# A hybrid residual block on one core: squares and scaling moved from GpSimd to ScalarE and VectorE, the memory heads' steps one chunk later

## The chip, the cores and the metric

The kernel runs on one core of one Trainium2 chip. A core has five engines, each with an instruction queue of its own that runs in order: TensorE (PE, matmuls into PSUM banks), VectorE (DVE, elementwise), ScalarE (ACT, elementwise with a function), GpSimd (POOL) and SyncE (SP, which here only issues DMAs). They wait for one another through semaphores. The metric is the device time of one execution in microseconds (us); lower is better.

## The reference, cut to what matters

One layer of a residual block, sequence 512, width 2048, float32, with 256 memory tokens. Only the parts that the change touches are spelled out.

```python
def rms_norm(x, g):
    return x * rsqrt(mean(x * x, -1) + 1e-6) * g

h = rms_norm(x, norm_g)                      # 512 x 2048
proj = h @ w_in                              # split into conv, latent attention, memory and gate columns
# branch A: short gated convolution; branch B: latent attention, 16 heads
# branch C: cross-attention into the memory tokens, 4 heads of width 256
q = rms_norm(mem_q.reshape(b, s, 4, 256), mem_qn_g)
k, v = split(rms_norm(mem, mem_norm_g) @ w_mem_kv, 2)
k = rms_norm(k.reshape(b, m, 4, 256), mem_kn_g)
p = softmax(einsum("bqhd,bmhd->bhqm", q, k) / 16)
mem_y = einsum("bhqm,bmhd->bqhd", p, v.reshape(b, m, 4, 256))
# every branch times silu(its gate columns), projected, merged by sigmoid gates, projected by w_o, added to x
```

## The kernel before, in words

Every float32 product is made of three matmuls on reduced-precision parts. A tile is split into `hi` (ScalarE, a copy to the reduced type) and `lo` (VectorE, the tile minus `hi`). `split` (L121) does this for activations, with a gain per partition folded in where there is one; `weights` (L137) does it for a weight chunk of 128x1024. `mm3` (L150) issues hi·hi, hi·lo and lo·hi. So PE cannot begin a chunk before ScalarE has made its `whi`, nor get beyond the first matmuls before VectorE has made its `wlo`. There are two `whi` and two `wlo` buffers and four raw weight buffers, so a `whi` also waits for PE to finish the chunk two places earlier.

**The front** is the stage from the start to the first latent projection. It computes the memory keys and values: four groups of eight weight chunks (32 chunks), each chunk 12 matmuls of 128x512. Three side jobs are woven in:

- In the first eight chunks `memory_chunk` (L248) loads two blocks of the memory tokens, splits them (tiles `mh` and `ml`), and calls `add_squares` (L236), which squares them (tile `sq`) and adds them up in `macc`. `memory_scale` (L261) turns `macc` into the tokens' scale.
- In chunks 6 to 13 `load_x` (L280) loads two blocks of x and adds their squares up in `xacc`.
- From chunk 17 on each step runs one step of `make_hT` (L287): a block of x times the row scale (tile `xs`, L304), then a `split` with the norm gain into the tile `hT`.

Before the change GpSimd squares the memory blocks (L242), adds both kinds of squares (L246) and makes `xs` (L304); ScalarE squares x (L244). GpSimd also takes every reciprocal root as a power of minus a half (L197, L269), on a few columns; these stay. In the front the order on SyncE is the program's; on the other engines the framework orders the instructions itself by a timeline model of its own. The same holds for the latent attention after it.

**The planned part**, from the second memory query group on, is ordered by hand. `drive` (L804) goes through a list of chunks. For each chunk number c it runs, in this order: the hooks set for c (`at`), the splits of the next chunks (`prep`, here for chunk c+1), the steps set for c (`phases`), the postponed pieces whose turn it is (`later`), and then chunk c's own matmuls. The emission order is the order on every engine.

Chunks 0 to 7 are the second memory query group, chunks 8 to 15 the first group of the memory gate, chunks 16 to 23 the second. `query_parts` (L1212) splits the four banks of a finished query group, squares them on ScalarE (`sq`, L1222) and adds the squares of a head on GpSimd (L1224). It is set for chunk 0 (heads 0 and 1) and chunk 8 (heads 2 and 3). `attention` (L1305) sets the steps of a pair of heads: `query_scales` (L1229, sums of `sq` by narrow matmuls at L1234, then the power on GpSimd) and `head_scores` (L1242) of the first head, its softmax as a postponed piece, `head_turn` (L1274, transposes of the softmax), `head_values` (L1287) together with the scores of the second head, and so on. With the pair set at chunk c, these run at c+1 to c+5. Results are copied (`my`) and stored to DRAM from ScalarE's queue one chunk later (L1301). At chunk 15 (`CLOSE`, `switch`, L1344) the memory heads' buffers are given up, and new tiles are laid over them, among them the `y` tiles that are loaded at chunk 15 (L1203 by way of L1326).

Of the kernel before, what the change touches and what calls it, by code (L numbers as in the profile page):

```python
# [20 lines left out]
AF = mybir.ActivationFunctionType  # L21
ALU = mybir.AluOpType
# [16 lines left out]
KC = 2  # L39
# [55 lines left out]
def body(ctx, tc, a, out):  # L95
    nc = tc.nc
    act, vec, pool = nc.scalar, nc.vector, nc.gpsimd
# [23 lines left out]
    def split(src, hi, lo, g=None):  # L121
        act.activation(hi, src, AF.Copy, scale=1.0 if g is None else g)  # L122
        if g is None:
            vec.tensor_tensor(out=lo, in0=src, in1=r32(hi), op=ALU.subtract)  # L124
        else:
            vec.scalar_tensor_tensor(out=lo, in0=src, scalar=g, in1=r32(hi),  # L126
                                     op0=ALU.mult, op1=ALU.subtract)
# [104 lines left out]
    macc = pst.tile([P, KC, M], F32, name="macc")  # L232
    xacc = pst.tile([P, KC, S], F32, name="xacc")
    mT = []

    def add_squares(c, t, acc, eng):  # L236

        sq = acc
        if c:
            sq = pst.tile(list(t.shape), F32, tag="sq", name="sq", bufs=2)  # L240
        if eng is pool:
            pool.tensor_tensor(out=sq, in0=t, in1=t, op=ALU.mult)  # L242
        else:
            act.activation(sq, t, AF.Square)  # L244
        if c:
            pool.tensor_tensor(out=acc, in0=acc, in1=sq, op=ALU.add)  # L246

    def memory_chunk(c):  # L248


        t = pst.tile([P, KC, M], F32, tag="mraw", name="mraw", bufs=4)
        nc.sync.dma_start(t, a["memT"][:, c * KC:(c + 1) * KC])
        for kk in range(KC):
            k = c * KC + kk
            hi = pmt.tile([P, M], F32R, name=f"mh{k}")
            lo = pmt.tile([P, M], F32R, name=f"ml{k}")
            split(t[:, kk], hi, lo, g(G_MEM + k))
            mT.append((hi, lo))
        add_squares(c, t, macc, pool)

    def memory_scale():  # L261
        b = bank("aux")
# [15 lines left out]
    xraws = []  # L278

    def load_x():  # L280
        c = len(xraws)
        t = pht.tile([P, KC, S], F32, tag="hT", name="xraw", bufs=KB + 1)
        nc.sync.dma_start(t, a["xT"][:, c * KC:(c + 1) * KC])
        xraws.append(t)
        add_squares(c, t, xacc, act)

    def make_hT():  # L287


        b = bank("aux")  # L290
        for i in range(NTB):
            for kk in range(KC):
                nc.tensor.matmul(b[:, i:i + 1], lhsT=xacc[:, kk, i * P:(i + 1) * P], rhs=one,
                                 start=kk == 0, stop=kk == KC - 1)
        r = rstd_of(b[:, :NTB], NTB, 1.0 / D, pst)
        rows = pst.tile([P, NTB, P], F32, name="xrows")
        vec.tensor_copy(rows, r.unsqueeze(2).to_broadcast([P, NTB, P]))
        b = transpose4([rows[:, i] for i in range(NTB)])
        scale = pst.tile([P, S], F32, name="xscale")
        act.activation(scale, b, AF.Copy)  # L300
        for k in range(KB):
            t = pht.tile([P, 2, S], F32R, tag="hT", name="hT", bufs=KB + 1)
            xs = pst.tile([P, S], F32, tag="xs", name="xs", bufs=2)
            pool.tensor_tensor(out=xs, in0=xraws[k // KC][:, k % KC], in1=scale, op=ALU.mult)  # L304
            split(xs, t[:, 0], t[:, 1], g(G_NORM + k))
            htiles.append(t)
            hT.append((t[:, 0], t[:, 1]))
            yield
# [5 lines left out]
    for grp in range(4):  # L314
# [12 lines left out]
        if grp < 2:  # L327
            krow = []
            for i, b in enumerate(banks):
                sq = pmt.tile([P, M], F32, tag="ksq", name="ksq")  # L330
# [9 lines left out]
            for f2 in range(2):  # L340
                b = bank("aux")
                for ff in range(2):
                    for i in range(2):
                        f = 2 * f2 + ff
                        nc.tensor.transpose(out=b[:, ff * M + i * P:ff * M + (i + 1) * P],
                                            in_=krow[i][:, f * P:(f + 1) * P], identity=ident)
                for ff in range(2):
                    f = 2 * f2 + ff
# [117 lines left out]
    for i, b in enumerate(banks):  # L466
        sq = pcr.tile([P, 512], F32, tag="csq", name="csq")
        ss = pcr.tile([P, 2], F32, tag="css2", name="css2", bufs=4)
        act.activation(sq[:, :288], b[:, :288], AF.Square, accum_out=ss[:, 0:1])
        t = pcr.tile([P, 512], F32, tag="crow", name="crow", bufs=4)  # L470
# [10 lines left out]
    for i, b in enumerate(banks):  # L481
        sq = pcr.tile([P, 512], F32, tag="csq", name="csq")
# [265 lines left out]
    plan, at, phases = [], defaultdict(list), defaultdict(list)  # L748
# [3 lines left out]
    def later(delay, us, fn):  # L752
        seq[0] += 1
        todo.append((now[0] + delay, seq[0], us, fn))
# [444 lines left out]
    mydram = dram.tile([8, P, S], F32, name="mydram")  # L1199
# [29 lines left out]
    def query_scales(grp):  # L1229

        b = bank(HEADS_IN[grp])
        for h in range(2):
            for i in range(NTB):
                nc.tensor.matmul(b[:, 4 * h + i:4 * h + i + 1], lhsT=heads[2 * grp + h]["sq"][:, i * P:(i + 1) * P],  # L1234
                                 rhs=one, start=True, stop=True)
        r = rstd_of(b[:, :8], 8, 1.0 / M, ppq)
        rs = ppq.tile([P, 8], F32, tag="rs", name="rs", bufs=2)
        vec.tensor_scalar(out=rs, in0=r, scalar1=MEM_SCALE, scalar2=None, op0=ALU.mult)
        for h in range(2):
            heads[2 * grp + h]["rs"] = rs[:, 4 * h:4 * h + 4]  # L1240

    def head_scores(head):  # L1242
        hd = heads[head]
        hd["p"] = []
        sbs = []
        for i2 in range(2):
            sb = bank(HEADS_IN[head // 2])
            for ii in range(2):
                cols = slice((2 * i2 + ii) * P, (2 * i2 + ii + 1) * P)
                for f in range(2):  # L1250
                    mm3(sb[:, ii * M:(ii + 1) * M], (hd["q"][f][0][:, cols], hd["q"][f][1][:, cols]),
                        mkT[2 * head + f], f == 0, f == 1)
            sbs.append(sb)

        def softmax(i2):
            sb, rs = sbs[i2], hd["rs"][:, 2 * i2:2 * i2 + 2]
            mx = ppq.tile([P, 2], F32, tag="mx", name="mx", bufs=2)
            vec.tensor_reduce(out=mx, in_=sb.rearrange("p (a b) -> p a b", a=2), op=ALU.max, axis=AX.X)
            nm = ppq.tile([P, 2], F32, tag="nm", name="nm", bufs=2)
            vec.scalar_tensor_tensor(out=nm, in0=mx, scalar=-1.0, in1=rs, op0=ALU.mult, op1=ALU.mult)  # L1260
            sm = ppq.tile([P, 2], F32, tag="sm", name="sm", bufs=2)
            p = ppq.tile([P, 2, M], F32, tag="p", name="p", bufs=2)
            for ii in range(2):
                act.activation(p[:, ii], sb[:, ii * M:(ii + 1) * M], AF.Exp, scale=rs[:, ii:ii + 1],
                               bias=nm[:, ii:ii + 1], accum_out=sm[:, ii:ii + 1])
            ri = ppq.tile([P, 2], F32, tag="ri", name="ri", bufs=2)
            vec.reciprocal(ri, sm)
            for ii in range(2):
                vec.tensor_scalar(out=p[:, ii], in0=p[:, ii], scalar1=ri[:, ii:ii + 1], scalar2=None, op0=ALU.mult)
                hd["p"].append(p[:, ii])  # L1270
        for i2 in range(2):
            later(0, 1.8, lambda i2=i2: softmax(i2))

    def head_turn(head):  # L1274
        hd = heads[head]
        bs = [transpose4([t[:, j * P:(j + 1) * P] for t in hd["p"]], HEADS_IN[head // 2]) for j in range(2)]
        hd["pt"] = []

        def parts_(j):
            hi = ppq.tile([P, S], F32R, tag=f"ph{j}", name=f"ph{j}")  # L1280
            lo = ppq.tile([P, S], F32R, tag=f"pl{j}", name=f"pl{j}")
            split(bs[j], hi, lo)
            hd["pt"].append((hi, lo))
        for j in range(2):
            later(0, 0.69, lambda j=j: parts_(j))

    def head_values(head):  # L1287
        hd, (grp, h) = heads[head], divmod(head, 2)
        bs = []
        for f in range(2):  # L1290
            yb = bank(HEADS_IN[grp])
            c0 = h * M + f * P
            for j in range(2):
                v = mv[j][grp]
                mm3(yb, (v[0][:, c0:c0 + P], v[1][:, c0:c0 + P]), hd["pt"][j], j == 0, j == 1)
            bs.append(yb)

        def put(f):
            y = ppq.tile([P, S], F32, tag="my", name="my", bufs=2)
            act.activation(y, bs[f], AF.Copy)  # L1300
            later(1, 0, lambda: nc.scalar.dma_start(mydram[2 * head + f], y))  # L1301
        for f in range(2):
            later(0, 0, lambda f=f: put(f))

    def attention(grp, c):  # L1305

        phases[c + 1] += [lambda: query_scales(grp), lambda: head_scores(2 * grp)]
        phases[c + 2] += [lambda: head_turn(2 * grp)]
        phases[c + 3] += [lambda: head_values(2 * grp), lambda: head_scores(2 * grp + 1)]
        phases[c + 4] += [lambda: head_turn(2 * grp + 1)]  # L1310
        phases[c + 5] += [lambda: head_values(2 * grp + 1)]

# [576 lines left out]
```

## Time and profile before

| | |
|---|---|
| median of 3 runs | 2176.95 us (2176.28 to 2177.11) |
| the profiled execution | 2177.01 us |
| its span, first to last instruction | 2175.2 us |
| TensorE clock granted, mean | 0.995 |
| HBM read and written | 269.41 MB and 48.23 MB |

So 1.8 us of the profiled execution lie outside the span. In the page, "busy" is time in which an engine executed something; in the list of groups, the time after the bar is idle time of that engine just before these instructions, and what ended it. A matmul's row shows a duration that includes its drain, so that neighbours overlap: the distance from start to start is what one costs when they follow one another.

### The profile page before, as it was taken

Reading aid. Unit: us, or ns where it says so; the run is one execution under the profiler, and the core shown is the slowest. Engines: PE = TensorE matmul, PEld = TensorE weight load, DVE = VectorE, ACT = ScalarE, POOL = GpSimd, SP = SyncE. Lnnn points to the kernel's source line nnn. Section 1 sums busy time; section 2 is a strip of 40 time slices with the busy share of each in tenths; the row PEclk is TensorE's granted clock in tenths of the full one; section 3 lists DMA queues with packets and bytes.
Section 4 is the critical chain, followed back from the end, with each engine's and each line's share of the span. In section 5 each row is a group of like instructions: output and inputs, shape, how many; then the busy total and the mean of one; then the engine's idle time right before and its main releaser. Section 6 shows DMA issues by size and latency. Waiting matters only on the chain.

```text
span 2175.2 us, 31867 instructions
## 1 busy us (share of the span) xinstructions
PE 2128.4 (98%) x12504; PEld 1893.9 (87%) x12504; DVE 1579.5 (73%) x2200; ACT 1028.1 (47%) x1551; POOL 216.2 (10%) x231
## 2 busy tenths in 40 slices
PE   7999999999999999999999999999999999999999
PEld 5788888888778999999999999888888888888887
DVE  7863777774335878788787776777777778867987
ACT  5533667675333444444444454444445434434433
POOL 7410311210001000000000000000000100111000
PEclk9999999999999999999999999999999999999999
DMA  7473212234227633333434433354344865487462
GB/s 263 159 257 108 88 49 74 68 135 166 70 78 225 205 116 106 120 105 107 141 126 175 164 121 113 117 174 145 98 154 144 282 213 186 147 276 214 152 190 94
DMA packets 110119, 322.35 MB, mean 148 GB/s; under 512 B 13200, under 2 KB 13456, under 8 KB 109968
## 3 DMA queue, kind: packets, MB, share of 16 engines
q1 hardware_dynamic: 78480, 253.89, 34.5%
q0 software_dynamic: 9888, 27.79, 4.7%
q10 hardware_dynamic: 21600, 38.63, 4.7%
q8 instruction: 98, 1.61, 0.3%
q14 instruction: 53, 0.43, 0.1%
HBM read 269.41 MB, written 48.23 MB: 146 GB/s over the span
## 4 chain that ended last, share of the span: by engine, by line
PE 88%; DVE 4%; ACT 3%; issue 2%; DMA 2%; POOL 1%; ACTq 0%; DVEq 0%; POOLq 0%
PE acc L154 15%; PE acc L153 15%; PE acc L155 15%; PE aux L154 13%; PE aux L153 13%; PE aux L155 13%; DVE wlo L147 1%; DVE wlo L124 1%; PE aux L660 1%; PE aux L204 1%; POOL xs L304 1%; ACT whi L122 0%; DVE hT L126 0%; ACT whi L146 0%; PE aux L640 0%
## 5 line engine op out<-in xcount | busy, mean ns | idle before, releaser
L124 DVE TENSOR_TENSOR wlo<-raw,whi 128x1024 fp32r<-128x1024 f32 x440 | 538.8, 1225 | 345.0 <-ACT whi L122 330.1
L122 ACT ACTIVATE whi<-raw 128x1024 fp32r<-128x1024 f32 x440 | 466.1, 1060 | 670.1 <-PE acc L154 159.9
L147 DVE TENSOR_TENSOR wlo<-raw,whi 128x1024 fp32r<-128x1024 f32 (+3 forms) x97 | 119.1, 1229 | 93.6 <-ACT whi L146 92.3
L146 ACT ACTIVATE whi<-raw 128x1024 fp32r<-128x1024 f32 (+3 forms) x97 | 92.7, 956 | 122.6 <-PE acc L155 43.4
L1203 POOL DMA_DIRECT2D y<-gdram x48 | 26.4, 550 | 1197.8 <-DMA gdram<-gy 954.9
L153 PE MATMUL acc<-whi,blk 128*128 128x512 f32 (+1 forms) x352 | 132.5, 380 | 2.0 <-DVE qt L585 1.4
L155 PE MATMUL acc<-whi,blk 128*128 128x512 f32 (+1 forms) x352 | 131.4, 374 | 0.0
L154 PE MATMUL acc<-wlo,blk 128*128 128x512 f32 (+1 forms) x352 | 131.1, 373 | 0.1
L1108 DVE TENSOR_TENSOR raw<-raw 128x1024 f32<-128x1024 f32 x96 | 116.9, 1218 | 0.0
L1018 DVE TENSOR_TENSOR raw<-raw 128x1024 f32<-128x1024 f32 x96 | 116.9, 1218 | 0.0
L122 ACT ACTIVATE whi<-s 128x1024 fp32r<-128x1024 f32 x64 | 67.9, 1062 | 93.9 <-PE acc L155 21.5
L153 PE MATMUL acc<-f,whi 128*128 128x256 f32 x384 | 108.7, 283 | 0.0
L154 PE MATMUL acc<-f,whi 128*128 128x256 f32 x384 | 108.7, 283 | 0.0
L155 PE MATMUL acc<-f,wlo 128*128 128x256 f32 x384 | 108.7, 283 | 0.0
L153 PE MATMUL aux<-f,whi 128*128 128x256 f32 x384 | 108.7, 283 | 0.0
L154 PE MATMUL aux<-f,whi 128*128 128x256 f32 x384 | 108.7, 283 | 0.0
L155 PE MATMUL aux<-f,wlo 128*128 128x256 f32 x384 | 108.7, 283 | 0.0
L154 PE MATMUL acc<-blk,whi 128*128 128x256 f32 (+1 forms) x320 | 97.6, 305 | 0.6 <-DVE blk L124 0.6
L153 PE MATMUL acc<-blk,whi 128*128 128x256 f32 (+1 forms) x320 | 97.8, 306 | 0.0
L153 PE MATMUL acc<-hU,whi 128*128 128x256 f32 (+1 forms) x320 | 97.5, 305 | 0.0
L153 PE MATMUL aux<-blk,whi 128*128 128x256 f32 (+1 forms) x320 | 97.5, 305 | 0.0
L153 PE MATMUL aux<-hU,whi 128*128 128x256 f32 (+1 forms) x320 | 97.4, 305 | 0.0
(458 smaller groups left out, 6322.0 us busy)
## 6 DMA issues: line engine op xcount, KB each, us to landing
raw<-in_w_conv SPq DMA_DIRECT2D x64, 512.0 KB, 4.3
raw<-in_w_mlaz SPq DMA_DIRECT2D x32, 512.0 KB, 4.8
raw<-in_w_gconv SPq DMA_DIRECT2D x32, 512.0 KB, 4.4
raw<-in_w_gmem SPq DMA_DIRECT2D x32, 512.0 KB, 3.4
raw<-in_w_gmla SPq DMA_DIRECT2D x32, 512.0 KB, 3.4
raw<-in_w_mla_out SPq DMA_DIRECT2D x32, 512.0 KB, 4.2
raw<-in_w_o SPq DMA_DIRECT2D x32, 512.0 KB, 4.0
raw<-in_w_mem_kv SPq DMA_DIRECT2D x31, 512.0 KB, 3.3
```

Of the source, the lines that this page charges most:

```text
L122: act.activation(hi, src, AF.Copy, scale=1.0 if g is None else g)
L124: vec.tensor_tensor(out=lo, in0=src, in1=r32(hi), op=ALU.subtract)
L146: act.activation(hi[:, cols], raw[:, cols], AF.Copy)
L147: vec.tensor_tensor(out=lo[:, cols], in0=raw[:, cols], in1=r32(hi[:, cols]), op=ALU.subtract)
L153: nc.tensor.matmul(o, lhsT=s[0], rhs=m[0], start=start, stop=False, skip_group_check=shared)
L154: nc.tensor.matmul(o, lhsT=s[0], rhs=m[1], start=False, stop=False, skip_group_check=shared)
L155: nc.tensor.matmul(o, lhsT=s[1], rhs=m[0], start=False, stop=stop, skip_group_check=shared)
L204: nc.tensor.transpose(out=b[:, i * P:(i + 1) * P], in_=s, identity=ident)
L304: pool.tensor_tensor(out=xs, in0=xraws[k // KC][:, k % KC], in1=scale, op=ALU.mult)
L1018: vec.tensor_tensor(out=o, in0=i0, in1=i1, op=op)
L1108: vec.tensor_tensor(out=o, in0=i0, in1=i1, op=op)
L1203: eng.dma_start(t, src)
```

## The change

- `add_squares` no longer takes an engine: ScalarE squares both the memory blocks and x, and VectorE adds to `macc` and `xacc`.
- `xs` in `make_hT` is made by VectorE.
- All steps of `attention` are set one chunk later: c+2 to c+6.
- The store of head 3's result is postponed by 0 instead of 1 chunk, so that it is still issued at chunk 14, ahead of the switch at chunk 15.

```diff
-    def add_squares(c, t, acc, eng):
+    def add_squares(c, t, acc):
         sq = acc
         if c:
             sq = pst.tile(list(t.shape), F32, tag="sq", name="sq", bufs=2)
-        if eng is pool:
-            pool.tensor_tensor(out=sq, in0=t, in1=t, op=ALU.mult)
-        else:
-            act.activation(sq, t, AF.Square)
+        act.activation(sq, t, AF.Square)
         if c:
-            pool.tensor_tensor(out=acc, in0=acc, in1=sq, op=ALU.add)
+            vec.tensor_tensor(out=acc, in0=acc, in1=sq, op=ALU.add)
...
-        add_squares(c, t, macc, pool)
+        add_squares(c, t, macc)
...
-        add_squares(c, t, xacc, act)
+        add_squares(c, t, xacc)
...
-            pool.tensor_tensor(out=xs, in0=xraws[k // KC][:, k % KC], in1=scale, op=ALU.mult)
+            vec.tensor_tensor(out=xs, in0=xraws[k // KC][:, k % KC], in1=scale, op=ALU.mult)
...
-            later(1, 0, lambda: nc.scalar.dma_start(mydram[2 * head + f], y))
+            later(0 if head == 3 else 1, 0, lambda: nc.scalar.dma_start(mydram[2 * head + f], y))
...
-        phases[c + 1] += [lambda: query_scales(grp), lambda: head_scores(2 * grp)]
-        phases[c + 2] += [lambda: head_turn(2 * grp)]
-        phases[c + 3] += [lambda: head_values(2 * grp), lambda: head_scores(2 * grp + 1)]
-        phases[c + 4] += [lambda: head_turn(2 * grp + 1)]
-        phases[c + 5] += [lambda: head_values(2 * grp + 1)]
+        phases[c + 2] += [lambda: query_scales(grp), lambda: head_scores(2 * grp)]
+        phases[c + 3] += [lambda: head_turn(2 * grp)]
+        phases[c + 4] += [lambda: head_values(2 * grp), lambda: head_scores(2 * grp + 1)]
+        phases[c + 5] += [lambda: head_turn(2 * grp + 1)]
+        phases[c + 6] += [lambda: head_values(2 * grp + 1)]
```

## The prediction

> **What bounds the kernel now.** I read the page first, then two stages closely: the front and the memory heads. The page's span and busy lines:
>
> ```profile
> span 2175.2 us, 31867 instructions
> PE 2128.4 (98%) x12504; PEld 1893.9 (87%) x12504; DVE 1579.5 (73%) x2200; ACT 1028.1 (47%) x1551; POOL 216.2 (10%) x231
> ```
>
> PE is busy for 98% of the span, so an edit pays only where PE waits or runs slowly. The view of stages gives the front, and around it and the heads the granted clock (the columns are the stretch, its length, busy time of PE, weight loads, DVE, ACT, POOL, then PEclk):
>
> ```profile
> 5.00:125.00 120.00, 103.13 (x432) 78.96 (x433) 102.25 (x98) 67.40 (x102) 75.33 (x44) 0.97 0.62 212
> 11.12:17.95 6.83, 3.73 (x15) 2.40 (x14) 6.83 (x6) 4.62 (x8) 6.67 (x6) 1.00 0.85 332
> 17.95:24.78 6.83, 5.11 (x12) 4.05 (x13) 6.83 (x5) 0.45 (x1) 6.67 (x5) 0.50 0.51 192
> 557.26:564.08 6.82, 3.32 (x18) 2.50 (x17) 2.25 (x3) 4.36 (x8) 1.77 (x2) 1.00 0.22 75
> 564.08:570.91 6.83, 6.02 (x28) 6.02 (x29) 2.64 (x5) 0.72 (x2) 2.42 (x2) 0.50 0.24 79
> ```
>
> In the front VectorE is busy for 102.25 us of 120, as much as PE. And each stretch in which PE was busy for only about half (3.73 and 3.32 us of 6.8) is followed by one at clock 0.50. A wait of PE costs twice.
>
> Groups of the front, then the same VectorE forms where GpSimd is idle (the last four rows):
>
> ```profile
> L154 PE MATMUL acc<-wlo,mh 128*128 128x512 f32 x128 | 54.1, 423 | 15.0 <-DVE wlo L147 15.0
> L147 DVE TENSOR_TENSOR wlo<-raw,whi 128x1024 fp32r<-128x1024 f32 x31 | 50.8, 1641 | 9.6 <-ACT whi L146 9.6
> L304 POOL TENSOR_TENSOR xs<-xraw,xscale 128x512 f32<-128x512 f32 x16 | 29.0, 1815 | 16.1 <-DVE hT L126 10.5 <-ACT xscale L300 5.6
> L126 DVE SCALAR_TENSOR_TENSOR hT<-xs,gains,hT 128x512 fp32r<-128x512 f32 x16 | 23.1, 1449 | 1.0 <-ACT hT L122 1.0
> L246 POOL TENSOR_TENSOR xacc<-xacc,sq 128x1024 f32<-128x1024 f32 x7 | 19.5, 2780 | 6.1 <-ACT sq L244 5.9
> L126 DVE SCALAR_TENSOR_TENSOR ml<-mraw,gains,mh 128x256 fp32r<-128x256 f32 x16 | 16.0, 1045 | 2.5 <-ACT mh L122 2.5
> ...
> L124 DVE TENSOR_TENSOR wlo<-raw,whi 128x1024 fp32r<-128x1024 f32 x440 | 538.8, 1225 | 345.0 <-ACT whi L122 330.1
> L147 DVE TENSOR_TENSOR wlo<-raw,whi 128x512 fp32r<-128x512 f32 x2 | 1.4, 686 | 0.2 <-ACT whi L146 0.2
> 29.19 0.87 DVE L126 SCALAR_TENSOR_TENSOR ml<-mraw,gains,mh 128x256 fp32r<-128x256 f32 x2
> 85.05 1.40 DVE L126 SCALAR_TENSOR_TENSOR hT<-xs,gains,hT 128x512 fp32r<-128x512 f32 x2
> ```
>
> PE waits 15.0 us for `wlo`. The three VectorE forms take 1641, 1449 and 1045 ns beside wide GpSimd work, and 1225, 700 and 435 ns without it. GpSimd's operations cost VectorE more time than they save it.
>
> **The front, part by part.** Relief on VectorE: 31 × (1.641 − 1.225) = 12.9 us, 16 × (1.449 − 0.70) = 12.0, 16 × (1.045 − 0.435) = 9.8; together 34.7. Added on VectorE: seven `macc` adds and sixteen `xs` of 128x512 at 0.686 (15.8 us), seven `xacc` adds of 128x1024 at 1.225 (8.6); together 24.4. Net 10.3 less: 102.25 becomes 92.
>
> What PE needs there:
>
> ```profile
> 5.94 0.80 PE L153 MATMUL acc<-whi,mh 128*128 128x512 f32 x1 [5.94 <-ACT whi L146]
> 11.20 0.63 PE L153 MATMUL acc<-whi,mh 128*128 128x512 f32 x2
> 34.94 0.95 PE L265 MATMUL aux<-one,macc 128*128 128x1 f32 x8
> 71.53 1.84 PE L293 MATMUL aux<-one,xacc 128*128 128x1 f32 x16
> 124.60 0.42 PE L153 MATMUL acc<-whi,hT 128*128 128x288 f32 x2
> 553.92 0.39 PE L153 MATMUL aux<-blk,whi 128*128 128x512 f32 x1
> 559.14 0.39 PE L155 MATMUL aux<-blk,wlo 128*128 128x512 f32 x1
> ```
>
> From the first matmul (5.94) to the first of the next stage (124.60) are 118.7 us. The last two rows are the first and the last of a chunk of 24 matmuls that run without a gap: 23 steps in 5.22 us, so 0.227 from start to start. A chunk of twelve costs 2.73 us, all 32 of them 87.3. Sums of squares take 0.95 + 1.84; some twenty transposes of 128 columns take about 2 (an estimate, at no more than the 0.12 that a matmul of 256 columns takes in the rows of the heads below). The first chunk took 5.26 us (5.94 to 11.20), 2.5 more than 2.73; I keep that, since the start-up doesn't change. PE's need is then 95 us, VectorE's 92. The second halved stretch (5.11 us busy at 0.50, so 2.6 lost) follows the waits for `wlo` and should go.
>
> So the ceiling is 118.7 − 95 = 24 us. It won't all come, and how much does is the widest unknown here, because the framework will order the front anew. Today the stage is 16 us longer than its busiest engine, because ScalarE, VectorE and GpSimd hand blocks round in order. One member of that ring goes, but VectorE gets an operation that must run between `wlo`s. I let the excess over the longer engine fall from 16 to 9: 104 us, a gain of **15 us**, with bounds of 5 and 24.
>
> ScalarE gains eight squares of 128x512 at 0.60 (row below), 4.8 us on 67.40 of 120; its idle third hides that, and without the cover a square would stand ahead of a `whi` at 0.6 each, 4.8 in all, inside my bounds. The narrow powers stay on GpSimd. What is late next is the pair `xs`–`hT` on VectorE.
>
> The Trainium skill's page "Perfetto Trace Analysis", section "Optimizing Scalar/DVE Operations", speaks against this edit: with a saturated DVE it advises moving work off it, even to GpSimd, though it adds that the two share a read port. By its first half the added 24.4 us would count in full; the solo rows above say the second half decides here. I keep the first as a rival.
>
> **The heads.** PE waits in group 0, and the chain that follows:
>
> ```profile
> 560.90 1.05 PE L1234 MATMUL acc<-one,sq 128*128 128x1 f32 x8 [1.38 <-POOL sq L1224]
> 562.89 0.60 ACT L1222 ACTIVATE sq<-acc 128x512 f32<-128x512 f32 x1 [0.82 <-DVE ql L126]
> 563.57 1.27 POOL L1224 TENSOR_TENSOR sq<-sq,sq 128x512 f32<-128x512 f32 x1 [2.72 <-ACT sq L1222]
> 564.89 1.86 PE L1234 MATMUL acc<-one,sq 128*128 128x1 f32 x8 [2.94 <-POOL sq L1224]
> 566.79 0.17 DVE L196 TENSOR_SCALAR rs_t<-acc 128x8 f32<-128x8 f32 x1 [0.88 <-PE acc L1234]
> 571.34 0.28 PE L155 MATMUL acc<-mkh,ql 128*128 128x256 f32 x1
> 571.46 0.40 PE L153 MATMUL aux<-blk,whi 128*128 128x512 f32 x1
> 574.92 0.62 DVE L1269 TENSOR_SCALAR p<-p,ri 128x256 f32<-128x256 f32 x2
> PE aux L1234 <- POOL sq L1224: 4.5, 2, 3.0
> PE acc L1234 <- POOL sq L1224: 4.3, 2, 2.9
> ```
>
> Chunk 0 (24 matmuls, 5.46 us) starts at 553.92 and ends its turn at 559.38; chunk 1 starts at 571.46, 12.08 us later. Between them lie two lots of eight narrow sums and 24 score matmuls. At full clock a lot takes about 1.0 (row at 560.90; 1.86 at half clock) and a score matmul 0.12 (571.34 to 571.46): 2.0 + 2.9 = 4.9 us. So 7.2 are waiting and halved clock.
>
> With the steps behind chunk 1, PE gets to them at 559.38 + 5.46 = 564.84. The last `sq` is summed at 563.57 + 1.27 = 564.84, and the first head's lot goes first: no wait. From the sums' end to the end of the softmax today's chain takes 566.79 to 575.54. Afterwards the sums end at the same time (564.84 + 2.0), but on VectorE the next chunk's `wlo` then stands ahead of `rs_t`: its `whi` can begin when PE leaves chunk 1 (564.84) and takes 1.05 (row under the rivals), the `wlo` 1.23, to 567.2. So the chain starts 0.4 later and ends at 575.9. PE comes to `head_turn` at 564.84 + 4.9 + 5.46 = 575.2 and waits 0.7. Net 6.5 in group 0. A wait of 0.7 leaves PE busy for nine tenths of a stretch, against the half that was followed by 0.50. Group 1 waited 4.5 against 4.3 and is built alike: the same 6.5. The heads give **13 us**, bounds 9.4 (turns that wait 2.5 each) and 14.4 (that wait for nothing).
>
> The late end, one chunk later, has cover:
>
> ```profile
> 668.91 1.80 SPq L1203 DMA_DIRECT2D y<-mydram  x4
> 674.30 0.81 ACTq L1301 DMA_DIRECT2D mydram<-my  x2
> 689.11 2.48 DVE L1332 TENSOR_TENSOR y<-acc,y 128x512 f32<-128x512 f32 x4 [0.48 <-ACT acc L1329]
> ```
>
> The `y` loads on SP wait for buffers that head 3 frees, now a chunk (5.46 us) later, at 674.4; behind them on SP stand weight loads of chunk 19 and on. Their use is at 689.11, so the shift is hidden, and would cost at most 5.46 if it weren't. Head 3's two stores move behind its own copies on ScalarE at about 675, not 674.30; behind them is a `whi` that waits for PE anyway. Cost nothing; no gain either.
>
> In the rows above, gaps of 1.38 and 2.94 us with narrow sums between them were followed by clock 0.50. The Trainium skill's page "TensorE: Matmul & The Clock Gate", section "Why this matters for your kernels", asks for no PE gaps over about 3 us and has a whole idle window halve the clock. By its letter neither gap would have done it, and the halving would have another cause; that is rival 4.
>
> **Sum.** 2177.0 − 15 − 13 = **2149 us**. The profiled execution (2177.01, of it 1.8 outside the span) and the median (2176.95) agree, so no correction.
>
> **The rivals.**
>
> 1. *VectorE becomes the front's bound.* If the order on it is strictly `xs`, wait for ScalarE's `hi`, `lo`, `wlo`, a step takes 0.69 + 0.72 + 0.70 + 1.23 = 3.3 to 3.4 us against PE's 2.73. In chunks 17 to 31 that is 15 × 3.4 = 51 us against 15 × 3.7 at today's mean (118.7/32), 4.5 less; to the other chunks I then give nothing. The front gains some 5: 2159. For it: 102.25 busy of 120. Against: the framework reorders there.
> 2. *Everything is gained*: 24 + 14 gives 2139. Needs both engines to overlap fully.
> 3. *The relief doesn't come*: VectorE's long times have another cause than GpSimd. Then 24.4 on 102.25 makes 127 us of VectorE from 5 on, an end near 132 instead of 124.6; some 8 lost, the heads' 13 gained: 2172. Against it: the solo rows. It is where the first half of the Trainium skill's advice in "Perfetto Trace Analysis" would lead.
> 4. *The halved clock in the heads stays*, because the gaps didn't cause it. Then the heads give the idle time alone, 4.3 + 4.5 less 1.4 at the turns, 7.4: 2155. Against it: at 564 it follows the gaps at once. It is the rule of the Trainium skill's page "TensorE: Matmul & The Clock Gate" by its letter.
> 5. *Slower: one ring.* Squares and adds join `whi`–`wlo` in a single file: ScalarE can't make the next `whi` before a piece that waits for VectorE.
>
> ```profile
> L146 ACT ACTIVATE whi<-raw 128x1024 fp32r<-128x1024 f32 x31 | 32.7, 1054 | 31.1 <-PE acc L155 24.9 <-DVE xrows L297 3.7 <-issue 1.6
> L122 ACT ACTIVATE hT<-xs,gains 128x512 fp32r<-128x512 f32 x16 | 11.5, 722 | 14.6 <-POOL xs L304 14.6
> L122 ACT ACTIVATE mh<-mraw,gains 128x256 fp32r<-128x256 f32 x16 | 7.2, 498 | 3.7 <-DMA mraw<-in_memT 3.7
> ```
>
> A step is 1.05 + 1.23 + 0.69 + 0.72 + 0.70 = 4.4 in chunks 17 to 31; 1.05 + 1.23 + 1.0 + 0.87 + 0.60 + 0.69 = 5.4 in the first eight; 1.05 + 1.23 + 1.05 + 1.23 = 4.6 in the six with a square and an add of x; 2.73 in the other three. That is 66 + 43 + 27 + 8 = 144 us, 26 more than today; less 13: 2190. It decides from a mean of (118.7 + 13)/32 = 4.1 us a chunk; today it is 3.7. The chance is small, since even today's ring of four engines runs faster.
>
> **Chances.** Forecast, with its own bounds from 2143 to 2156, 0.60; rival 1 0.18; rival 2 0.09; rival 3 0.04; rival 4 0.04; rival 5 0.05. A difference under 0.2% (4.4 us) is what a measurement of this kernel can hardly tell from none. Faster 0.93, within 0.2% 0.02 (half of rival 3), slower 0.05. The range runs from rival 2's edge, 2140, over rival 1 to 2162.
>
> **What would show it.** Right: no wide GpSimd rows before 125 us; `wlo`, `ml` and `hT` near 1225, 435 and 700 ns; the first latent matmul near 110; no 0.50 at 564 or 629, and waits under 1 us at the head turns. Wrong: VectorE nearly gapless with PE still waiting for `wlo`; chunks over 4.1 us; a wait of PE at L1234; a new wait at the switch near 680.

## The result, and the profile after

| | before | changed |
|---|---|---|
| median | 2177.03 us (2176.28 to 2180.82, 4 runs) | 2143.39 us (2141.56 to 2144.38, 4 runs) |
| ratio | | 0.9841, 95% interval 0.9824 to 0.9858 |
| the profiled execution's span | 2175.2 us | 2142.4 us |

33.6 us less by the medians, 32.8 by the spans; 28 were predicted. The page's first lines of the changed kernel:

```profile
span 2142.4 us, 31861 instructions
PE 2117.1 (99%) x12504; PEld 1889.9 (88%) x12504; DVE 1565.1 (73%) x2230; ACT 1031.4 (48%) x1559; POOL 146.4 (7%) x193
```

GpSimd lost 69.8 us of busy time, and VectorE, which took most of that work over, became 14.4 us less busy. The groups of the front and two rows of PE's timeline (its first matmul, and the first of the next stage) say how. The line numbers are the changed kernel's, three lower from L243 on:

```profile
L154 PE MATMUL acc<-wlo,mh 128*128 128x512 f32 x128 | 51.4, 402 | 2.0 <-DVE wlo L147 2.0
L147 DVE TENSOR_TENSOR wlo<-raw,whi 128x1024 fp32r<-128x1024 f32 x31 | 37.9, 1221 | 9.2 <-ACT whi L146 9.0
L126 DVE SCALAR_TENSOR_TENSOR hT<-xs,gains,hT 128x512 fp32r<-128x512 f32 x16 | 11.6, 745 | 0.0
L301 DVE TENSOR_TENSOR xs<-xraw,xscale 128x512 f32<-128x512 f32 x16 | 10.7, 684 | 0.0
L243 DVE TENSOR_TENSOR xacc<-xacc,sq 128x1024 f32<-128x1024 f32 x7 | 8.5, 1218 | 0.7 <-ACT sq L241 0.7
L126 DVE SCALAR_TENSOR_TENSOR ml<-mraw,gains,mh 128x256 fp32r<-128x256 f32 x16 | 7.0, 478 | 2.3 <-ACT mh L122 2.2
L243 DVE TENSOR_TENSOR macc<-macc,sq 128x512 f32<-128x512 f32 x7 | 4.8, 683 | 0.1
...
6.50 0.80 PE L153 MATMUL acc<-whi,mh 128*128 128x512 f32 x1 [6.50 <-ACT whi L146]
104.64 0.42 PE L153 MATMUL acc<-whi,hT 128*128 128x288 f32 x2
```

Read the means: `wlo` fell from 1641 to 1221 ns, `hT` from 1449 to 745, `ml` from 1045 to 478. The operations that came over cost what the prediction took for them (684, 683, 1218). PE's wait for `wlo` fell from 15.0 to 2.0 us, and the first matmul of the next stage came at 104.64 instead of 124.60: 20.0 us.

The stages, in the form of the prediction's view (length, busy PE, weight loads, DVE, ACT, POOL, then PEclk); the first row is the front, the other two are spoken of below:

```profile
5.00:104.64 99.64, 96.02 (x428) 77.90 (x429) 85.17 (x119) 69.72 (x108) 6.43 (x6) 1.00 0.72 253
1960.30:1967.14 6.84, 4.27 (x27) 3.48 (x27) 6.09 (x11) 2.75 (x5) 1.09 (x2) 1.00 0.54 156
1967.14:1970.55 3.41, 3.41 (x11) 2.74 (x10) 3.34 (x7) 2.07 (x5) 1.09 (x2) 0.50 0.63 208
```

PE is busy for 96.02 of the front's 99.64 us and VectorE for 85.17. So the stage is now hardly longer than PE's own work.

The heads, in PE's and VectorE's timelines: the last matmul of chunk 1, the first of chunk 2, the first transposes, then the last steps of the softmax chain.

```profile
544.68 0.39 PE L155 MATMUL aux<-blk,wlo 128*128 128x512 f32 x1
549.58 0.40 PE L153 MATMUL aux<-blk,whi 128*128 128x512 f32 x1
555.05 1.03 PE L204 MATMUL acc<-ident,p 128*128 128x128 f32 x8
549.16 0.17 DVE L1235 TENSOR_SCALAR rs<-rs_r 128x8 f32<-128x8 f32 x1 [1.84 <-POOL rs_r L197]
549.24 0.68 DVE L1255 TENSOR_REDUCE mx<-acc 128x2 f32<-128x512 f32 x1
554.60 0.62 DVE L1266 TENSOR_SCALAR p<-p,ri 128x256 f32<-128x256 f32 x2
```

From the end of one chunk's turn (544.68 + 0.23) to the next chunk are 4.67 us instead of 12.08, with no wait at the narrow sums. In the second pair it is 4.67 as well, against 11.8. Together 14.5 us.

20.0 + 14.5 = 34.5 us, of which the end of the span shows 32.8. The lead shrank near the end, where PE waits for ScalarE's copies before the last transposes: the matmul that started at 1996.03 in the kernel before starts at 1961.49 (34.5 earlier), the one of 2010.09 at 1977.91 (32.2 earlier). Some 0.6 came back by the end. The first row is the kernel before's list of waits, the second the changed kernel's:

```profile
PE acc L1704 <- ACT hU L1718: 1.8, 1, 1.8
```

```profile
PE acc L1701 <- ACT hU L1715: 2.6, 1, 2.6
```

The wait is 0.8 us longer. The rows of 1960 and 1967 above show it as a stretch with PE busy for 4.27 of 6.84 us, and behind it 3.4 us at clock 0.50. Another profiled execution of the same changed kernel, e8 below, had 1.8 here again and no halving, so this loss varies from one execution to the next and isn't bound to the change.

### The profile page after: what moved, and what is told of

It is laid out like the page before. It is cut to its first block, busy times and chain, and to the rows that moved or that the text cites. A ratio compares the mean times of both kernels' runs of the same rounds, so it can differ in the third digit from the quotient of the medians.

```text
span 2142.4 us, 31861 instructions
## 1 busy us (share of the span) xinstructions
PE 2117.1 (99%) x12504; PEld 1889.9 (88%) x12504; DVE 1565.1 (73%) x2230; ACT 1031.4 (48%) x1559; POOL 146.4 (7%) x193
## 4 chain that ended last, share of the span: by engine, by line
PE 92%; DVE 3%; ACT 2%; DMA 1%; issue 1%; POOL 0%; ACTq 0%; DVEq 0%; POOLq 0%
PE acc L154 16%; PE acc L153 16%; PE acc L155 16%; PE aux L154 13%; PE aux L155 13%; PE aux L153 13%; PE aux L657 1%; PE aux L204 1%; DVE wlo L124 0%; ACT whi L146 0%; PE aux L637 0%; PE aux L638 0%; PE aux L639 0%; DMA mraw<-in_memT 0%; PE aux L641 0%
## 5 line engine op out<-in xcount | busy, mean ns | idle before, releaser
L124 DVE TENSOR_TENSOR wlo<-raw,whi 128x1024 fp32r<-128x1024 f32 x440 | 538.6, 1225 | 336.1 <-ACT whi L122 329.0
L147 DVE TENSOR_TENSOR wlo<-raw,whi 128x1024 fp32r<-128x1024 f32 (+3 forms) x97 | 106.1, 1094 | 90.1 <-ACT whi L146 88.5
L1105 DVE TENSOR_TENSOR raw<-raw 128x1024 f32<-128x1024 f32 x96 | 116.9, 1218 | 0.0
L1015 DVE TENSOR_TENSOR raw<-raw 128x1024 f32<-128x1024 f32 x96 | 116.9, 1218 | 0.0
```

The lines of the kernel that those rows point to most:

```text
L147: vec.tensor_tensor(out=lo[:, cols], in0=raw[:, cols], in1=r32(hi[:, cols]), op=ALU.subtract)
L1015: vec.tensor_tensor(out=o, in0=i0, in1=i1, op=op)
L1105: vec.tensor_tensor(out=o, in0=i0, in1=i1, op=op)
```

## The experiments

The theory: GpSimd's operations that read SBUF lengthen VectorE's operations with two inputs in SBUF, and that relief is what the front gained; the heads gained their waits and the halved clock behind them; the two parts don't depend on each other. Main rival: the front gained because GpSimd left the chain of handoffs, so that its latency and not its traffic was the cost.

**One part at a time.** e1 is the kernel before with the heads' steps one chunk later, e2 the changed kernel with the heads as before:

```diff
 # e2, against the changed kernel
-            later(0 if head == 3 else 1, 0, lambda: nc.scalar.dma_start(...))
+            later(1, 0, lambda: nc.scalar.dma_start(...))
...
-        phases[c + 2] += [lambda: query_scales(grp), lambda: head_scores(2 * grp)]
+        phases[c + 1] += [lambda: query_scales(grp), lambda: head_scores(2 * grp)]
...
```

> The kernel before with the memory heads' steps one chunk later and nothing else. Theory (the heads gained the waits at the narrow sums and the halved clock behind them, independently of the front): the front ends at 124.6 us as before, no waits at L1234, no clock 0.50 near 564 and 629; the distance between the two chunks falls from 12.1 and 11.8 to 4.7 us each, 14.5 us in all: 2162.5 us. Rival (the halved clock has another cause and stays): 7 to 8 us, 2169.

> The changed kernel with the heads' steps as before. Theory (the two parts are independent): the front ends at 104.6 us, 20 earlier than before, the heads keep 12.1 and 11.8 us: 2157 us. Rival (part of the front's gain is given back later, as waits on loads that were hidden): less than 18 us, over 2159.

e1 took 2162.76 us (ratio to before 0.9922, 0.9905 to 0.9938), e2 2158.14 (0.9902, 0.9887 to 0.9917). Chunk to chunk and the clock in e1 (PE's timeline, then a stretch), then e2's front end, its waits, and the clock behind them:

```profile
567.98 0.39 PE L155 MATMUL aux<-blk,wlo 128*128 128x512 f32 x1
572.87 0.40 PE L153 MATMUL aux<-blk,whi 128*128 128x512 f32 x1
570.00:576.00 6.00, 6.00 (x39) 5.47 (x39) 2.76 (x9) 1.20 (x4) 1.66 (x1) 1.00 0.52 175
```

```profile
104.66 0.42 PE L153 MATMUL acc<-whi,hT 128*128 128x288 f32 x2
PE aux L1231 <- POOL sq L1221: 4.5, 2, 3.0
PE acc L1231 <- POOL sq L1221: 4.3, 2, 2.9
542.61:549.44 6.83, 4.47 (x21) 4.47 (x22) 2.12 (x4) 1.54 (x2) 2.92 (x2) 0.50 0.23 80
610.87:617.70 6.83, 5.93 (x28) 5.94 (x29) 2.69 (x5) 0.67 (x2) 2.49 (x2) 0.50 0.21 77
```

In e1 the distance is 4.66 us with the clock at 1.00, though the front is the old one (its end at 126.3, 1.7 later than in the profile before; the expectation had 124.6). In e2 the front ends at 104.66 with the old waits of 4.5 and 4.3 in the heads, and behind them the clock is at 0.50 again (chunk to chunk 12.5 and 12.2 us; 12.1 and 11.8 were expected). By ratios the parts save 0.78% and 0.98%, 1.76% together, against 1.59% (1.42 to 1.76) for the whole: independent, as far as a measurement tells. The halved clock in the heads goes with the waits (e1) and comes with them (e2, some 20 us earlier than in the kernel before), which leaves little room for another cause.

**Which GpSimd work cost it.** e3 puts `xs` alone back on GpSimd, e4 the memory squares and all adds alone:

```diff
 # e3
-            vec.tensor_tensor(out=xs, in0=xraws[k // KC][:, k % KC], in1=scale, op=ALU.mult)
+            pool.tensor_tensor(out=xs, in0=xraws[k // KC][:, k % KC], in1=scale, op=ALU.mult)
...
 # e4
-        add_squares(c, t, macc)
+        add_squares(c, t, macc, pool)     # add_squares as before: squares and adds on GpSimd
...
```

> The changed kernel with xs alone back on GpSimd. Theory (GpSimd's reads slow VectorE down): hT back from 745 to about 1450 ns, some of the wlo of chunks 17 to 31 over 1.8 us, and these chunks as slow as before, 54 us where they now take 45: 2152 us. Rival (the squares were the whole gain): 2143 to 2145.

> The changed kernel with the squares of the memory tokens and all adds back on GpSimd, xs on VectorE. Theory: ml back to about 1045 ns, the wlo of chunks 1 to 4 and 8 to 13 over 2 us; chunk 16 ends at 70 instead of 59.4 us: 2154 us. Rival (xs was the whole gain): 2143 to 2145.

e3 took 2151.60 us (0.9872, 0.9857 to 0.9887), e4 2155.47 (0.9888, 0.9873 to 0.9902). Groups and the front's end, e3 first:

```profile
L126 DVE SCALAR_TENSOR_TENSOR hT<-xs,gains,hT 128x512 fp32r<-128x512 f32 x16 | 23.1, 1449 | 1.0 <-ACT hT L122 1.0
113.03 0.42 PE L153 MATMUL acc<-whi,hT 128*128 128x288 f32 x2
```

```profile
L147 DVE TENSOR_TENSOR wlo<-raw,whi 128x1024 fp32r<-128x1024 f32 x31 | 47.5, 1535 | 10.5 <-ACT whi L146 10.4
L126 DVE SCALAR_TENSOR_TENSOR ml<-mraw,gains,mh 128x256 fp32r<-128x256 f32 x16 | 16.5, 1073 | 2.2 <-ACT mh L122 2.2
117.94 0.42 PE L153 MATMUL acc<-whi,hT 128*128 128x288 f32 x2
```

Each set of GpSimd operations lengthens the VectorE operations that run beside it (`hT` 1449 in e3; `ml` 1073 and `wlo` 1535 in e4) and costs its own stage: the front ends 8.4 and 13.3 us later than 104.64. These two don't tell traffic from handoffs yet; the next does.

**Traffic or handoffs.** e5 is the changed kernel with GpSimd operations that nobody waits for; e6 has writes without reads.

```diff
 # e5
+                pool.tensor_tensor(out=junk[:, 0, :M], in0=r32(hi), in1=r32(hi), op=op)          # twice behind each mh
...
+        pool.tensor_tensor(out=junk, in0=t, in1=t, op=ALU.add)                                 # behind each load of x
...
+            pool.tensor_tensor(out=junk[:, 1], in0=r32(t[:, 0]), in1=r32(t[:, 0]), op=ALU.mult)  # behind each hT
...
 # e6
+            for _ in range(2):
+                pool.memset(xraws[k // KC][:, k % KC], 0.0)                                     # behind each xs
```

> The changed kernel with GpSimd operations added in the front whose results nobody reads: two of 128x256 on each mh, one of 128x1024 on each block pair of x, one of 128x512 on each hT, all reading SBUF into a scratch tile, each paced by the engine that wrote its input and waited for by none. Theory (GpSimd's reads make VectorE's two-input operations longer): wlo, ml, hT and xs grow to 1.5 to 2 times, VectorE has 20 to 34 us more to do and bounds the front; it ends at 125 to 138 us: 2163 to 2177. Rival (the gain came from taking GpSimd out of the chain of handoffs): nobody waits for GpSimd, so nothing changes: 2143.

> The changed kernel with two GpSimd memsets of 128x512 behind each xs, on the block of x that was just used up (it is not read again): writes without reads, paced by VectorE. If only GpSimd's reads slow VectorE's two-input operations: hT stays near 745, xs near 685 ns: 2143 us. If any wide GpSimd operation does: both grow to 1.4 times or more in chunks 17 to 31, and the front ends 8 us later or more: 2151.

e5 took 2173.19 us (0.9972, 0.9962 to 0.9982), 30 more than the changed kernel. Its groups, the front and its end, PE's wait for `wlo`, and of its waits all that wait for GpSimd:

```profile
L258 POOL TENSOR_TENSOR junk<-mh 128x256 f32<-128x256 f32 x32 | 30.4, 950 | 7.0 <-ACT mh L122 4.6
L147 DVE TENSOR_TENSOR wlo<-raw,whi 128x1024 fp32r<-128x1024 f32 x31 | 46.6, 1505 | 7.6 <-ACT whi L146 7.6
L126 DVE SCALAR_TENSOR_TENSOR hT<-xs,gains,hT 128x512 fp32r<-128x512 f32 x16 | 17.8, 1135 | 0.0
L305 DVE TENSOR_TENSOR xs<-xraw,xscale 128x512 f32<-128x512 f32 x16 | 15.7, 998 | 0.0
5.00:134.63 129.63, 106.27 (x428) 81.05 (x429) 116.97 (x121) 70.55 (x107) 77.65 (x60) 0.95 0.57 199
134.63 0.36 PE L153 MATMUL acc<-whi,hT 128*128 128x288 f32 x1
PE acc L154 <- DVE wlo L147: 21.7, 16, 3.6
DVE kn L339 <- POOL rs_r L197: 3.0, 3, 1.4
DVE xrows L298 <- POOL rs_r L197: 1.1, 1, 1.1
```

The results are thrown away, and the only waits for GpSimd are those for the narrow powers, 4.1 us (3.3 in the changed kernel, for the same two users). Yet `wlo`, `hT` and `xs` take 1505, 1135 and 998 ns instead of 1221, 745 and 684 (`wlo` and `xs` less than the 1.5 to 2 times that were expected). PE waits 21.7 us for `wlo` instead of 2.0, its clock falls to 0.95 in the mean, and the front ends 30 us later. GpSimd is busy there for 77.65 us, about as long as in the kernel before (75.33). The handoff rival falls: the traffic alone can cost the whole of the front's gain. Nor is it the order that the framework chose: in e5 VectorE, ScalarE and PE run through the front in the changed kernel's order but for a few pieces.

e6 took 2143.96 us (0.9835, 0.9822 to 0.9849), the changed kernel's time:

```profile
L304 POOL MEMSET xraw<- 128x512 f32 x32 | 16.7, 528 | 26.3 <-DVE xs L301 15.2 <-issue 3.7 <-ACT mvh L122 2.7
L126 DVE SCALAR_TENSOR_TENSOR hT<-xs,gains,hT 128x512 fp32r<-128x512 f32 x16 | 11.6, 746 | 0.0
L301 DVE TENSOR_TENSOR xs<-xraw,xscale 128x512 f32<-128x512 f32 x16 | 10.7, 685 | 0.0
```

With 16.7 us of GpSimd writes among them `hT` and `xs` keep 746 and 685 ns, in the changed kernel's order. e5's operations read and write, e6's only write: it is GpSimd's reads that cost, as far as a memset can stand for the writes.

**The wait near the end.** The changed kernel's longest wait of PE after the start is the 2.6 us above. e7 sets the last turn of the merged sums one chunk later; e8 is the changed kernel once more, as its neighbour on the same chip.

```diff
-    ASKED, TURNED = (0, 3, 7, 11), (3, 7, 10, 13)
+    ASKED, TURNED = (0, 3, 7, 11), (3, 7, 10, 14)
```

> The changed kernel with the last turn of the merged sums one chunk later (14 instead of 13). Theory (the wait of 2.6 us at the last transposes and the halved clock behind it come from ScalarE's copies that stand behind a busy stretch of VectorE): the wait goes, 2.6 + 1.7 us less at most: 2139 to 2142. Rival (the forms made from these sums come late in turn): the wait moves behind, 2143 to 2147.

> The changed kernel itself on this chip, as the base of its neighbours: 2143 us, front ended at 104.6 us.

e7 took 2139.37 us (2138.53 to 2140.18; 0.9817, 0.9803 to 0.983), e8 2142.80 (2141.82 to 2143.30; 0.9831, 0.9818 to 0.9845). Their runs don't overlap, so e7 is about 3.4 us faster than the changed kernel, the fastest version here, though the intervals of the two ratios do overlap. In e7 PE waits for nothing there and the clock stays up; e8 still waits (e7's stretch first, then e8's wait):

```profile
1960.00:1970.00 10.00, 10.00 (x54) 8.49 (x54) 9.14 (x16) 3.43 (x6) 2.19 (x4) 1.00 0.65 186
```

```profile
PE acc L1701 <- ACT hU L1715: 1.8, 1, 1.8
```

The wait explains only a part. The matmul that starts at 1976.39 in e8, just behind the wait, starts at 1972.95 in e7, 3.4 us earlier; 2.1 of them arise at the wait. e7 was 1.4 ahead before it, 0.8 of that from the front, which the edit doesn't touch; this part may be chance.

## Why the prediction was right, point by point

- **The relief.** Right in kind and nearly in size: `wlo` and `hT` came to 1221 and 745 ns (taken: 1225 and 700), `ml` to 478 (taken: 435). The 700 and 435 were half the length of a pair of rows that overlap, so a single one is some 45 ns longer. VectorE's front was put at 92 us; it measured 85.17, in a stretch 20 us shorter (99.64 instead of 120) that ends before the last two `xs` and `hT`.
- **How much of the front's ceiling comes.** This is the term that was mis-sized. The excess over the busier engine was to fall from 16 to 9 us; from first matmul to next stage the changed kernel takes 98.1 us (6.50 to 104.64) against PE's need of 95, so it fell to 3, and the gain was 20.0 instead of 15. What I had held back for went away: `xs` on VectorE stood in nobody's way, the stretch of chunks 17 to 31 runs without a wait but one, and the second halved clock is gone too. GpSimd's traffic alone suffices for the waits that I extrapolated from, as e5 shows; handing blocks round isn't needed for them.
- **ScalarE's squares.** Costed at nothing, rightly: PE's wait for `whi` beyond the start is nil in the changed kernel.
- **The heads.** 13 were predicted, 14.5 measured, near the upper bound of 14.4. The steps cost 4.67 instead of 4.9 us. The wait of 0.7 at the turn didn't come: the softmax was done at 555.22, PE came at 555.05, and its first transposes need the first half only. The chain was put 0.7 us too long (from `rs_t` to the end of the softmax 8.06 us now, 8.75 before), mostly since the old one held a wait of 0.6 of VectorE for PE before `mx` (it began at 569.56, `rs` was ready at 568.96), and now `mx` follows `rs` at once.
- **The late end.** Right: no wait of PE between 520 and 680 in the changed kernel.
- **Not foreseen.** The 1.7 us that are missing at the end, by a wait that I hadn't listed and the halved clock behind it. The kernel before had the wait as well, with 1.8. That this profile had the long form of it was chance. Without that loss the larger gains of the front and the heads would have shown in full; as it is, 2143.4 lies at the edge of the forecast's own bounds.
- **The rivals.** VectorE as the bound (1) is refuted by PE's wait for `wlo`, 2.0 us in all; no relief (3) by the groups and e5; the halved clock from another cause (4) by e1 and e2; the ring (5) by the mean of 98.1/32 = 3.1 us a chunk, where it needed 4.1. The truth lay between the forecast and rival 2.

## What to carry to other kernels

A saturated engine can be relieved by giving it more work, if that work now slows it down from an engine beside it: compare the mean of one instruction form where the neighbour runs and where it doesn't before splitting work over the two. Look at the granted clock behind each long wait of PE: where it halved here, the loss was well over the wait itself (7.2 us for waits of 4.3 in the first pair of heads). And steps that depend on a chain longer than a chunk belong behind the next chunk; what hides the chain is then PE's own work.

## What the runs showed of the hardware

How the two engines share, in the kernel before, VectorE first and GpSimd second; the last pair is an operation of VectorE whose data comes from PSUM:

```profile
101.01 1.21 DVE L147 TENSOR_TENSOR wlo<-raw,whi 128x1024 fp32r<-128x1024 f32 x1
102.14 1.77 DVE L126 SCALAR_TENSOR_TENSOR hT<-xs,gains,hT 128x512 fp32r<-128x512 f32 x1
101.16 2.21 POOL L304 TENSOR_TENSOR xs<-xraw,xscale 128x512 f32<-128x512 f32 x1 [1.82 <-DVE hT L126]
...
96.19 0.74 DVE L126 SCALAR_TENSOR_TENSOR mvl<-acc,mr,mvh 128x512 fp32r<-128x512 f32 x1
95.21 2.21 POOL L304 TENSOR_TENSOR xs<-xraw,xscale 128x512 f32<-128x512 f32 x1 [0.62 <-DVE hT L126]
```

`wlo` began 0.15 us before `xs` and kept its solo time of 1.21; `xs` took 2.21. The `hT` that came up next took 1.77: about the 1.0 to 1.2 until `xs` was done, and its own 0.74. That looks like turns of whole instructions rather than half speed for both. The Trainium skill's page "SBUF — State Buffer", section "Who interferes with whom", states an exclusive lock, and that a VectorE instruction with two SBUF inputs contends with a GpSimd instruction that reads SBUF, but not with one that only writes it. The rows of `hT` and `xs` agree with the first and e6's 746 ns with the second. `mvl`, with one input in PSUM, ran in 0.74 beside `xs`.

Near the end, 0.8 us more of waiting went with a halved clock. Of the nine profiled executions that have the wait for `hU`, three (the changed kernel, e2, e3) waited 2.6 us and then ran 3.4 us at 0.50; the other six, e8 with the same kernel among them, waited 1.8 and kept the full clock.
